# A buffer of its own for the early store, and one plan for both groups, in a top-2 dispatch kernel

## The chip, the cores and the metric

The kernel runs on one core of a Trainium2 chip. The metric is the time of one execution on the device in microseconds (us). Its data lie in the chip's main memory (DRAM); the core computes on its on-chip memory of 128 partitions. VectorE (DVE in the profile) does the element-wise arithmetic, ScalarE (ACT) the sigmoid. Transfers are issued by SyncE (SP) and ScalarE and carried by 16 DMA engines, which all of them share.

## The reference

There are 16 x 1024 = 16384 tokens, each with 512 values in `x` and 8 router logits, all 32-bit floats, and k is 2. Per token the two largest logits are taken, their softmax weights are normalised to sum to one, and the token's row is written out twice, once with each weight, the second largest first:

```python
    logits_max = np.max(router_logits, axis=-1, keepdims=True)
    probs = np.exp(router_logits - logits_max)
    probs = probs / np.sum(probs, axis=-1, keepdims=True)
    topk_indices = np.argsort(probs, axis=-1)[..., -k:]
    topk_probs = np.take_along_axis(probs, topk_indices, axis=-1)
    topk_probs = topk_probs / np.sum(topk_probs, axis=-1, keepdims=True)
    x_expanded = x[:, :, np.newaxis, :].repeat(k, axis=2)
    return (x_expanded * topk_probs[..., np.newaxis]).astype(np.float32)
```

So 33.6 MB of `x` and 0.5 MB of logits come in and 67.1 MB go out; the experts' indices are not returned. With two weights that sum to one, they are the sigmoids of plus and minus the difference of the two largest logits.

## The kernel before

**Tiling.** Each of the 128 partitions takes 128 tokens ("rows" from here on), in two groups of 65 and 63 rows (`GROUPS`, L49). A row of `x` is 2 KB per partition, a row of output 4 KB. The buffer `xs` (L95) holds one group of `x`, 65 rows; the buffer `osp` (L96) holds 16 rows of output (L = 16, h = 8). `logits` (L94) and the small tiles of the tournament in `top2_weights` have buffers of their own.

**Loads.** SyncE issues a group's loads in the pieces that `LOADS` gives (L112): 2, 4, 2, 8, 17 and 32 rows in the first group, 16, 16 and 31 in the second. After the first 6 rows it issues two loads of logits for both groups (L116, L117), and there the program puts the tournament: VectorE finds the largest and second largest of 8 logits by halving (L27 to L37), subtracts them (L40), and ScalarE makes the two weights (L42, L43).

**Multiplications and stores.** For each block of the plan VectorE multiplies `n` rows by their two weights into the block's output place (L128), and a DMA stores it (L136). In the first group the blocks are rows 0 to 1 and 2 to 15 in `osp`, 16 to 31 in `xs`, 32 to 39 and 40 to 47 in the halves of `osp`, then 48 to 56 and 57 to 64 in `xs` (`LAST`, L54). In the second: 0 to 15 in `osp`, 16 to 31 in `xs`, 32 to 39 and 40 to 47 in `osp`, 48 to 62 in `xs`. The block of two rows is stored from ScalarE's queue, "the early store", all others from SyncE's.

**Output written over the input.** A block that is "over" (L98 to L104) puts its output into `xs` itself, in the place of rows that have been used: n rows of output take the room of 2n rows of input. With `a = 2 * r - G` the place of rows 48 to 56 of group 0 is `xs[31:49]`, that of rows 57 to 64 is `xs[49:65]`; the second block (rows 16 to 31) is given G = 32, so it lies in `xs[0:32]`.

**Order.** There is no loop of fixed depth and no planner's due time: every engine and every queue takes its work in the order of the program, and a framework puts a wait wherever a region is read before it is written, written before it was read, or reused before its store has landed. A wait of SyncE holds up all transfers that are programmed behind it, and the second group's loads stand behind the first group's stores.

Of the kernel before, what the change touches and what calls it, by code (L numbers as in the profile page):

```python
# [1 line left out]

# [4 lines left out]

F32 = mybir.dt.float32
ALU = mybir.AluOpType
ACTF = mybir.ActivationFunctionType  # L10
P = 128


def top2_weights(nc, pool, logits, M, E, tag=""):

    hi, lo, n = None, None, E  # L20
    while n > 1:
        n //= 2
        if hi is None:
            a, b = logits[:, :, 0:n], logits[:, :, n : 2 * n]
            nhi = pool.tile([P, M, n], F32, tag=f"hi{n}{tag}")
            nlo = b
            nc.vector.tensor_tensor(nhi, a, b, op=ALU.max)  # L27
            nc.vector.tensor_tensor(nlo, a, b, op=ALU.min)  # L28
        else:
            a, b = hi[:, :, 0:n], hi[:, :, n : 2 * n]  # L30
            nhi = pool.tile([P, M, n], F32, tag=f"hi{n}{tag}")
            nlo = pool.tile([P, M, n], F32, tag=f"lo{n}{tag}")
            tmp = pool.tile([P, M, n], F32, tag=f"tmp{n}{tag}")
            nc.vector.tensor_tensor(tmp, lo[:, :, 0:n], lo[:, :, n : 2 * n], op=ALU.max)  # L34
            nc.vector.tensor_tensor(nlo, a, b, op=ALU.min)  # L35
            nc.vector.tensor_tensor(nlo, nlo, tmp, op=ALU.max)  # L36
            nc.vector.tensor_tensor(nhi, a, b, op=ALU.max)  # L37
        hi, lo = nhi, nlo
    dlt = pool.tile([P, M], F32, tag=f"dlt{tag}")
    nc.vector.tensor_tensor(dlt, hi[:, :, 0], lo[:, :, 0], op=ALU.subtract)  # L40
    WA = pool.tile([P, M, 2], F32, tag=f"WA{tag}")
    nc.scalar.activation(WA[:, :, 0], dlt, ACTF.Sigmoid, scale=-1.0)  # L42
    nc.scalar.activation(WA[:, :, 1], dlt, ACTF.Sigmoid, scale=1.0)  # L43
    return WA

GROUPS = [65, 63]  # L49

LOADS = [[2, 4, 2, 8, 17, 32], [16, 16, 31]]


LAST = [[(48, 9), (57, 8)], [(48, 15)]]  # L54


@with_exitstack
def kernel(
    ctx: ExitStack,
    tc: tile.TileContext,  # L60
    x: bass.AP,
    router_logits: bass.AP,
    k: bass.AP,
    out: bass.AP,
):
    nc = tc.nc
    B, S, D = x.shape
    E = router_logits.shape[-1]
    N = B * S
    assert int(k) == 2 and E == 8 and N == P * sum(GROUPS)  # L70
    M = N // P

    L = 16
    x_v, o_v, rl_v = [], [], []
    t0 = 0
    for n in GROUPS:
        t1 = t0 + P * n
        x_v.append(
            x.rearrange("b s d -> (b s) d")[t0:t1].rearrange("(p m) d -> p m d", p=P)
        )  # L80
        o_v.append(
            out.rearrange("b s k d -> (b s) k d")[t0:t1].rearrange(
                "(p m) k d -> p m k d", p=P
            )
        )
        rl_v.append(
            router_logits.rearrange("b s e -> (b s) e")[t0:t1].rearrange(
                "(p m) e -> p m e", p=P
            )
        )  # L90
        t0 = t1

    wpool = ctx.enter_context(tc.tile_pool(name="wpool", bufs=1))
    logits = wpool.tile([P, M, E], F32)  # L94
    xs = wpool.tile([P, max(GROUPS), D], F32)  # L95
    osp = wpool.tile([P, L, 2, D], F32)  # L96

    def over(r, n, G):  # L98

        a = 2 * r - G
        return xs[:, a : a + 2 * n, :].rearrange("p (r k) d -> p r k d", k=2)  # L104

    h = L // 2
    e = 2
    m0 = 0
    for g, G in enumerate(GROUPS):
        r = 0  # L110
        for n in LOADS[g]:
            nc.sync.dma_start(xs[:, r : r + n, :], x_v[g][:, r : r + n, :])  # L112
            r += n
            if g == 0 and r == 6:

                nc.sync.dma_start(logits[:, :G], rl_v[0])  # L116
                nc.sync.dma_start(logits[:, G:], rl_v[1])  # L117
                WA = top2_weights(nc, wpool, logits, M, E)
        assert r == G
        begin = [(0, e, osp[:, :e]), (e, L - e, osp[:, e:])] if g == 0 else [(0, L, osp)]  # L120
        plan = begin + [
            (L, L, over(L, L, 2 * L)),
            (2 * L, h, osp[:, :h]),
            (2 * L + h, h, osp[:, h:]),
        ]
        plan += [(r, n, over(r, n, G)) for r, n in LAST[g]]
        for r, n, og in plan:
            nc.vector.tensor_tensor(  # L128
                og,
                xs[:, r : r + n, :].unsqueeze(2).to_broadcast([P, n, 2, D]),  # L130
                WA[:, m0 + r : m0 + r + n, :].unsqueeze(3).to_broadcast([P, n, 2, D]),
                op=ALU.mult,
            )

            queue = nc.scalar if n == e else nc.sync
            queue.dma_start(o_v[g][:, r : r + n], og)  # L136
        m0 += G


# [1 line left out]
_INS = ['x', 'router_logits', 'k']  # L141
_OUTS = [((16, 1024, 2, 512), 'float32')]

_NUMBERS = {'k': 2}


# [26 lines left out]
```

## Time and profile before

| | |
|---|---|
| Three timed runs | 240.04, 240.05, 240.24 us; median 240.05 us |
| Profiled execution: its own time, as the page gives it (span) | 238.5 us |
| Median less this span (what lies around it) | 1.55 us |
| VectorE busy | 142.0 us, 60%, 23 instructions |
| of these, the multiplications (L128) | 69.1 us into `osp`, 69.1 us into `xs` |
| DMA packets | 3312, 101.19 MB, mean 424 GB/s over the span |
| Waits of VectorE for loads of `x` / for stores from `osp` / from `xs` | 31.2 / 30.1 / 2.0 us |

The page gives the span of the profiled execution, from its first instruction to its last, and no other time of that execution; the timed runs are other executions of the same kernel. The page cuts the span into 40 slices and gives for each the busy share of each engine in tenths, the mean busy share of the 16 DMA engines and what they moved. Transfers are listed by their queue: q1 holds those that SyncE issues, q10 the one that ScalarE issues. "To landing" is the time from the issue to the moment at which the last of a transfer's packets has arrived and its semaphore is set. A queue like SPq in the timeline shows the issuing instruction, not the movement of the data.

### The profile page before, as it was taken

The page shows a single profiled execution, that of the slowest core. Times are in us where ns is not written, and L with a number is a line of the kernel's source. Part 1 is how long each engine was busy: PE and PEld are TensorE (multiplying, and loading weights), DVE is VectorE, ACT ScalarE, POOL GpSimd, SP SyncE. Part 2 cuts the span into 40 slices and gives each one's busy share as a digit, 9 for nine tenths or more (in the row PEclk, how much of TensorE's full clock was granted, in tenths as well). Part 3 has the DMA queues.
Part 4 walks back from the last instruction along what each step waited for, and adds up shares of the span by engine and source line. Part 5 has one row for each costly group of instructions (what it writes and reads, how often), then busy time and mean ns, then how long its engine had stood idle before and what let it go on. Part 6 is the DMA issues. An engine that isn't in the chain of part 4 may idle for free.

```text
span 238.5 us, 116 instructions
## 1 busy us (share of the span) xinstructions
DVE 142.0 (60%) x23; ACT 1.8 (1%) x3; POOL 0.2 (0%) x4
## 2 busy tenths in 40 slices
DVE  0599999900299699900000699999006999990000
ACT  2000000000000000000000000000000000000000
POOL 0000000000000000000000000000000000000000
DMA  7999989899898999999999999998999989999994
GB/s 261 434 470 411 459 383 528 330 462 462 352 506 352 440 440 440 440 414 465 440 429 434 412 478 458 394 495 374 462 418 429 451 363 429 440 440 429 495 453 206
DMA packets 3312, 101.19 MB, mean 424 GB/s; under 512 B 368, under 2 KB 496, under 8 KB 880
## 3 DMA queue, kind: packets, MB, share of 16 engines
q1 hardware_dynamic: 3168, 100.14, 97.8%
q10 hardware_dynamic: 144, 1.05, 1.0%
HBM read 34.08 MB, written 67.11 MB: 424 GB/s over the span
## 4 chain that ended last, share of the span: by engine, by line
DMA 43%; DVE 41%; issue 4%; SPq 1%; ACT 0%; DVEq 0%
DVE xs L128 22%; DVE osp L128 18%; DMA out_dram<-xs 15%; DMA xs<-in_x_dram 13%; DMA out_dram<-osp 13%; DMA logits<-in_router_logits_dram 3%; SPq L112 0%; DVE nhi L27 0%; DVE logits L28 0%; DVE nlo L36 0%; DVE nhi L37 0%; DVE tmp L34 0%; DVE nlo L35 0%; SPq L116 0%; SPq L136 0%
## 5 line engine op out<-in xcount | busy, mean ns | idle before, releaser
L128 DVE TENSOR_TENSOR osp<-xs,WA 128x8192 f32<-128x8192 f32 (+3 forms) x7 | 69.1, 9908 | 61.9 <-DMA xs<-in_x_dram 31.2
L128 DVE TENSOR_TENSOR xs<-xs,WA 128x16384 f32<-128x16384 f32 (+3 forms) x5 | 69.1, 13812 | 2.2 <-DMA out_dram<-xs 2.0
L27 DVE TENSOR_TENSOR nhi<-logits 128x512 f32<-128x512 f32 x1 | 0.7, 691 | 8.3 <-DMA logits<-in_router_logits_dram 8.3
L42 ACT ACT_TABLE_LOAD x1 | 1.3, 1283 | 0.7 <-PEq L154 0.7
L28 DVE TENSOR_TENSOR logits<-logits 128x512 f32<-128x512 f32 x1 | 0.7, 692 | 0.0
L37 DVE TENSOR_TENSOR nhi<-nhi 128x256 f32<-128x256 f32 (+1 forms) x2 | 0.7, 351 | 0.0
L35 DVE TENSOR_TENSOR nlo<-nhi 128x256 f32<-128x256 f32 (+1 forms) x2 | 0.7, 350 | 0.0
L36 DVE TENSOR_TENSOR nlo<-nlo,tmp 128x256 f32<-128x256 f32 (+1 forms) x2 | 0.7, 350 | 0.0
L34 DVE TENSOR_TENSOR tmp<-logits 128x256 f32<-128x256 f32 x1 | 0.4, 418 | 0.0
L42 ACT ACTIVATE WA<-dlt 128x128 f32<-128x128 f32 x1 | 0.3, 315 | 10.2 <-DVE dlt L40 10.2
L40 DVE TENSOR_TENSOR dlt<-nhi,nlo 128x128 f32<-128x128 f32 x1 | 0.3, 291 | 0.0
L43 ACT ACTIVATE WA<-dlt 128x128 f32<-128x128 f32 x1 | 0.3, 297 | 0.0
L34 DVE TENSOR_TENSOR tmp<-nlo 128x128 f32<-128x128 f32 x1 | 0.3, 283 | 0.0
L154 POOL MEMSET const-bfloat16-1.0<- 128x1 bf16 x1 | 0.1, 101 | 0.0
L154 POOL MEMSET const-uint8-127<- 128x1 uint8 x1 | 0.1, 101 | 0.0
L154 POOL MEMSET const-float32-0.0<- 128x1 f32 x1 | 0.1, 98 | 0.2 <-issue 0.2
L154 POOL MEMSET const-float32-1.0<- 128x1 f32 x1 | 0.1, 98 | 0.0
## 6 DMA issues: line engine op xcount, KB each, us to landing
out_dram<-osp SPq DMA_DIRECT2D x4, 4096.0 KB, 20.7
xs<-in_x_dram SPq DMA_DIRECT2D x2, 4096.0 KB, 29.9
xs<-in_x_dram SPq DMA_DIRECT2D x1, 7936.0 KB, 38.0
out_dram<-xs SPq DMA_DIRECT2D x1, 7680.0 KB, 23.2
out_dram<-osp SPq DMA_DIRECT2D x1, 7168.0 KB, 33.9
out_dram<-xs SPq DMA_DIRECT2D x1, 4608.0 KB, 20.4
xs<-in_x_dram SPq DMA_DIRECT2D x1, 4352.0 KB, 22.4
out_dram<-xs SPq DMA_DIRECT2D x1, 4096.0 KB, 21.5
```

What stands on the lines that cost most here:

```text
L27: nc.vector.tensor_tensor(nhi, a, b, op=ALU.max)
L28: nc.vector.tensor_tensor(nlo, a, b, op=ALU.min)
L34: nc.vector.tensor_tensor(tmp, lo[:, :, 0:n], lo[:, :, n : 2 * n], op=ALU.max)
L35: nc.vector.tensor_tensor(nlo, a, b, op=ALU.min)
L36: nc.vector.tensor_tensor(nlo, nlo, tmp, op=ALU.max)
L37: nc.vector.tensor_tensor(nhi, a, b, op=ALU.max)
L40: nc.vector.tensor_tensor(dlt, hi[:, :, 0], lo[:, :, 0], op=ALU.subtract)
L42: nc.scalar.activation(WA[:, :, 0], dlt, ACTF.Sigmoid, scale=-1.0)
L43: nc.scalar.activation(WA[:, :, 1], dlt, ACTF.Sigmoid, scale=1.0)
L128: nc.vector.tensor_tensor(og, xs[:, r : r + n, :].unsqueeze(2).to_broadcast([P, n, 2, D]), WA[:, m0 + r : m0 + r + n, :].unsqueeze(3).to_b ...
L154: nc = _bacc.Bacc("TRN2", target_bir_lowering=False, num_devices=1)
```

## The change

It touches buffers, the cut of the first group's loads, and the plan of the first group's blocks.

- The early store's two rows are written to a new buffer `oe` of two rows. `EARLY = [2, 0]` says how many such rows a group has; `LAST` is gone.
- The other 63 rows of the first group have the blocks of the second group, moved by two: rows 2 to 17 in all 16 rows of `osp`, 18 to 33 in `xs`, 34 to 41 and 42 to 49 in the halves of `osp`, 50 to 64 in `xs`, which makes six stores instead of seven.
- `over` gives its block the place `xs[r - n : r + n]`: `xs[2:34]` for rows 18 to 33, `xs[35:65]` for rows 50 to 64. In the second group the places are those of before.
- The first group's loads are 2, 4, 2, 10, 15 and 32 rows instead of 2, 4, 2, 8, 17 and 32.
- `logits` and the tournament's small tiles are cut out of the front of `osp` by `room`; `dlt` and `WA` have buffers of their own. The tournament's instructions are the same.

```diff
-LOADS = [[2, 4, 2, 8, 17, 32], [16, 16, 31]]
+LOADS = [[2, 4, 2, 10, 15, 32], [16, 16, 31]]
-LAST = [[(48, 9), (57, 8)], [(48, 15)]]
+EARLY = [2, 0]
...
-    logits = wpool.tile([P, M, E], F32)
     xs = wpool.tile([P, max(GROUPS), D], F32)
     osp = wpool.tile([P, L, 2, D], F32)
-    def over(r, n, G):
-        a = 2 * r - G
-        return xs[:, a : a + 2 * n, :].rearrange("p (r k) d -> p r k d", k=2)
+    oe = wpool.tile([P, max(EARLY), 2, D], F32)
+    WA = wpool.tile([P, M, 2], F32)
+    dlt = wpool.tile([P, M], F32)
+    flat = osp.rearrange("p l k d -> p (l k d)")
+    taken = [0]
+    def room(n):
+        o = taken[0]
+        taken[0] += M * n
+        return flat[:, o : o + M * n].rearrange("p (m n) -> p m n", n=n)
+    logits = room(E)
+    def over(r, n):
+        return xs[:, r - n : r + n, :].rearrange("p (r k) d -> p r k d", k=2)
...
-                WA = top2_weights(nc, wpool, logits, M, E)
+                top2_weights(nc, WA, dlt, room, logits, E)
...
-        begin = [(0, e, osp[:, :e]), (e, L - e, osp[:, e:])] if g == 0 else [(0, L, osp)]
-        plan = begin + [
-            (L, L, over(L, L, 2 * L)),
-            (2 * L, h, osp[:, :h]),
-            (2 * L + h, h, osp[:, h:]),
+        e = EARLY[g]
+        plan = [(0, e, oe, nc.scalar)] if e else []
+        plan += [
+            (e, L, osp, nc.sync),
+            (e + L, L, over(e + L, L), nc.sync),
+            (e + 2 * L, h, osp[:, :h], nc.sync),
+            (e + 2 * L + h, h, osp[:, h:], nc.sync),
+            (e + 3 * L, G - e - 3 * L, over(e + 3 * L, G - e - 3 * L), nc.sync),
         ]
-        plan += [(r, n, over(r, n, G)) for r, n in LAST[g]]
-        for r, n, og in plan:
+        for r, n, og, queue in plan:
...
-            queue = nc.scalar if n == e else nc.sync
             queue.dma_start(o_v[g][:, r : r + n], og)
```

More of the change, by code (lines that the diff above doesn't have):

```diff
@@ L11, with top2_weights @@
 P = 128
-def top2_weights(nc, pool, logits, M, E, tag=""):
+def top2_weights(nc, WA, dlt, room, logits, E):
+    tt = nc.vector.tensor_tensor
     hi, lo, n = None, None, E
@@ L24, in top2_weights @@
             a, b = logits[:, :, 0:n], logits[:, :, n : 2 * n]
[L25 to L28, printed above, removed]
+            nhi, nlo = room(n), b
+            tt(nhi, a, b, op=ALU.max)
+            tt(nlo, a, b, op=ALU.min)
         else:
             a, b = hi[:, :, 0:n], hi[:, :, n : 2 * n]
[L31 to L37, printed above, removed]
+            nhi, nlo, tmp = room(n), room(n), room(n)
+            tt(tmp, lo[:, :, 0:n], lo[:, :, n : 2 * n], op=ALU.max)
+            tt(nlo, a, b, op=ALU.min)
+            tt(nlo, nlo, tmp, op=ALU.max)
+            tt(nhi, a, b, op=ALU.max)
         hi, lo = nhi, nlo
-    dlt = pool.tile([P, M], F32, tag=f"dlt{tag}")
-    nc.vector.tensor_tensor(dlt, hi[:, :, 0], lo[:, :, 0], op=ALU.subtract)
-    WA = pool.tile([P, M, 2], F32, tag=f"WA{tag}")
+    tt(dlt, hi[:, :, 0], lo[:, :, 0], op=ALU.subtract)
     nc.scalar.activation(WA[:, :, 0], dlt, ACTF.Sigmoid, scale=-1.0)
     nc.scalar.activation(WA[:, :, 1], dlt, ACTF.Sigmoid, scale=1.0)
-    return WA
 GROUPS = [65, 63]
-LOADS = [[2, 4, 2, 8, 17, 32], [16, 16, 31]]
-LAST = [[(48, 9), (57, 8)], [(48, 15)]]
+LOADS = [[2, 4, 2, 10, 15, 32], [16, 16, 31]]
+EARLY = [2, 0]
 @with_exitstack
@@ L93 @@
     wpool = ctx.enter_context(tc.tile_pool(name="wpool", bufs=1))
-    logits = wpool.tile([P, M, E], F32)
     xs = wpool.tile([P, max(GROUPS), D], F32)
     osp = wpool.tile([P, L, 2, D], F32)
-    def over(r, n, G):
-        a = 2 * r - G
-        return xs[:, a : a + 2 * n, :].rearrange("p (r k) d -> p r k d", k=2)
+    oe = wpool.tile([P, max(EARLY), 2, D], F32)
[10 more added lines that the diff above has]
+        return xs[:, r - n : r + n, :].rearrange("p (r k) d -> p r k d", k=2)
     h = L // 2
-    e = 2
     m0 = 0
```

## The prediction

> **What bounds the kernel now.** I first read the page's slices and queues, to see which resource has no holes.
>
> ```profile
> DMA  7999989899898999999999999998999989999994
> GB/s 261 434 470 411 459 383 528 330 462 462 352 506 352 440 440 440 440 414 465 440 429 434 412 478 458 394 495 374 462 418 429 451 363 429 440 440 429 495 453 206
> q1 hardware_dynamic: 3168, 100.14, 97.8%
> q10 hardware_dynamic: 144, 1.05, 1.0%
> ```
>
> The reader is to see that the 16 DMA engines are full in every slice but the first and the last: the packets of q1 (SyncE's queue) and q10 (ScalarE's) fill 98.8% of the span. VectorE is busy for only 60%. All 101.19 MB go through those engines whatever the order, so the end moves only if an engine runs dry, or if the packets get slower. The chain of waits, with its 41% DVE, misleads here: it names who released whom, not what was scarce.
>
> Next the waits of VectorE, to know its slack.
>
> ```profile
> DVE osp L128 <- DMA xs<-in_x_dram: 31.2, 1, 31.2
> DVE osp L128 <- DMA out_dram<-osp: 30.1, 2, 16.7
> DVE xs L128 <- DMA out_dram<-xs: 2.0, 1, 2.0
> ```
>
> These 63.3 us are VectorE waiting for a transfer while the queue is full, so removing one is worth nothing by itself. The question is how late VectorE may hand over each store before the queue drains; that I read from the timeline.
>
> ```profile
> 0.73 0.86 SPq L112 DMA_DIRECT2D xs<-in_x_dram  x2
> 2.58 2.22 SPq L112 DMA_DIRECT2D xs<-in_x_dram  x4
> 12.75 17.29 DVE L128 TENSOR_TENSOR osp<-xs,WA 128x2048 f32<-128x2048 f32 x2 [0.58 <-ACT WA L43]
> 15.08 0.37 ACTq L136 DMA_DIRECT2D out_dram<-osp  x1
> 30.07 0.35 SPq L136 DMA_DIRECT2D out_dram<-osp  x1
> 30.08 17.23 DVE L128 TENSOR_TENSOR xs<-xs,WA 128x16384 f32<-128x16384 f32 x1
> 47.33 0.34 SPq L136 DMA_DIRECT2D out_dram<-xs  x1
> 64.02 17.29 DVE L128 TENSOR_TENSOR osp<-xs,WA 128x8192 f32<-128x8192 f32 x2 [16.71 <-DMA out_dram<-osp]
> ```
>
> The store of rows 2 to 15 is issued at 30.07 and the next at 47.33. Last come the issues by size, and stretches of 0.1 us (start and end, length, busy times, clock, DMA share, GB/s), in which a packet counts whole where it starts.
>
> ```profile
> xs<-in_x_dram SPq DMA_DIRECT2D x1, 42.6
> ```
>
> ```profile
> 1.70:1.80 0.10, 0.00 (x0) 0.10 (x1) 0.00 (x0) 1.00 1.47 205
> 43.20:43.30 0.10, 0.10 (x1) 0.00 (x0) 0.00 (x0) 1.00 13.30 4588
> 43.30:43.40 0.10, 0.10 (x1) 0.00 (x0) 0.00 (x0) 1.00 5.86 1966
> 43.40:43.50 0.10, 0.10 (x1) 0.00 (x0) 0.00 (x0) 1.00 7.81 2621
> 43.50:43.60 0.10, 0.10 (x1) 0.00 (x0) 0.00 (x0) 1.00 3.77 1311
> ...
> 46.10:46.20 0.10, 0.10 (x1) 0.00 (x0) 0.00 (x0) 1.00 1.33 573
> ...
> 46.60:46.70 0.10, 0.10 (x1) 0.00 (x0) 0.00 (x0) 1.00 2.66 1147
> ```
>
> Each transfer is 128 packets, 8 for each engine, so the engines move in waves of 16. The last wave of the 32-row load starts between 43.2 and 43.6; its shares add up to 30.74 tenths of a us, 3.07 us for each packet. The first wave of the store behind it starts between 46.1 and 46.7. The queue is thus served in order, without a gap. The load was the last of the four issues that end at 4.80 (2.58 + 2.22), so it was issued near 4.37 and landed near 46.97, 0.3 us after its last packet.
>
> **The change part by part.** The sums are made on the profiled execution, with its span of 238.5 us. The three timed runs have a median of 240.05 us, 1.55 us more, which lies around the span; I add the difference in span to the median.
>
> *Scratch and logits in the buffer osp.* The same 11 VectorE instructions on the same shapes (0.28 to 0.69 us each, 8.28 to 12.17): no cost. Were the shared buffer to bring waits between them, at worst an instruction's length each, about 4.5 us, the chain would end near 17; that delays the first big store from about 32.9 to 37.4, and the load keeps the queue full until 46. Nothing either way.
>
> *Two rows to a buffer of their own.* The 2.29 us instruction and the ScalarE store at 15.08 stay. Nobody waits for this store any more; before, the instruction at 64.02 did, beside the later store that ended its wait. Nothing.
>
> *Loads of 10 and 15 rows for 8 and 17.* As many DMAs. The 8-row load landed near 14.3 (11.0 us after an issue near 3.4); two rows more, 0.52 MB at 434 GB/s, put the 10-row load at 15.5. The next multiplication starts 0.5 us later than 15.04. It now has 16 rows (17.23 us by the 128x16384 row) instead of 14 (15.09), so its store is issued at 32.8 and not at 30.07. The cover is again the load, to 46.1. Nothing.
>
> *One store fewer.* Seven stores of group 0 become six: 9 and 8 rows turn into one of 15, 14 into 16, 8 + 8 stay. The bytes are equal. What goes is 8 packets and a semaphore packet on every engine. From the waves in the trace (64 KB packets 2.416 us, those of an 8-row store at 83.6 to 84.2 1.214) a packet costs 2 x 1.214 - 2.416 = 0.012 us beyond its bytes: 8 x 0.012, about 0.1 us gained. SyncE issues one 0.33 us DMA less, off the path.
>
> *The 2.0 us wait at 83.3 goes.* The last block, xs[35:65], no longer overlaps the earlier in-place block, xs[2:34]. The queue was full there, so nothing; group 1's first loads are issued near 100 and no longer at 102.30 and near 113, behind a queue that is full to 122. Nothing.
>
> *A new wait.* This is the one that matters. The second 16-row block was rows 16 to 31 and is now rows 18 to 33. The loads end at rows 2, 6, 8, 18, 33, 65: row 33 comes with the 32-row load, where before row 31 came with the 17-row one. The 17.23 us instruction that started at 30.08 now waits until 46.97. Behind it on VectorE are all other multiplications of the group, behind its store on SyncE all other stores. It starts 0.09 us after the landing (as 83.27 to 83.36 in the chain), ends at 64.29, and SyncE issues at 64.30 instead of 47.33.
>
> What is in the queue until then: the 16-row store, issued at 32.8, starts at 46.1 to 46.7 and has 8 waves. A wave of 64 KB packets costs 2.41 us (those of the present 16-row store start at 63.1, 65.5 and 67.9), 19.3 in all, so the engines run dry between 65.4 and 66.0. When does the new store's data start? The lower bound is the first load on this same SyncE queue: issued at 0.73, first packets at 1.70, 0.97 us, and 14 packets within 0.35 us. The upper bound is ScalarE's store, issued at 15.08, whose first packet shows at 18.6, 3.5 us; but there the engines were busy with packets of 1.26 us, of which one or two lay ahead. I take 0.97, since the queue and the idle engine match. Data starts from 65.27 on the first engine to 65.62 on the last. The engine that drains first idles up to 0.2 us, the one that drains last, which sets the end, has 0.4 to 0.7 us to spare. Cost 0 to 0.2 us at 0.97; at 3.5 us data starts at 67.8, and the slowest engine loses 1.8 us.
>
> The Trainium skill's page "DMA: Bandwidth & Descriptors", section "Anatomy of one DMA", speaks against this hand-over: it gives a DMA a fixed cost of about 2.0 us, mostly at its completion. The trace has 0.3 + 0.97 = 1.3 us for landing and start here, 0.7 less. By the page an estimate puts the data near 66.0 and the cost at 0.3 us; by the row it is 0.1.
>
> Afterwards the queue has cover again: the next 8-row block waits for the first big store (66.4), is issued at 75.1, and the store begun at 65.6 lasts to 85. The last 15-row store goes out at 99.9 with 8-row stores queued to 104.8. Group 1 has the same plan, and its first load, queued behind the same bytes, lands as before. Sum: +0.2 - 0.1 = +0.1 us; predicted 240.2 us.
>
> **The rivals.**
>
> *The queue runs dry (slower).* Place: 65.4 to 67.8. It decides once a store needs more than about 1.7 us from issue to data (0.97 plus the slowest engine's spare 0.7); each us beyond that is a us at the end, as no later stretch is idle enough to win it back. ScalarE's 3.5 us speak for it, the first load's 0.97 against. At 3.5 us the end moves by 1.8 (less 0.1): 241.8; midway, at 2.5 us, 0.8 less 0.1: 240.8.
>
> *The stretched wave disappears (faster).* The last wave of the 32-row load took 3.07 us, its predecessor (40.8) 2.42, and the last one of group 1's load (158.0) about 2.4. If the 0.65 us comes from the sizes queued around it, the new load sizes and the 16-row store may lose it: 239.4. Against it: this load and the store's kind stay.
>
> *The change does less than it says.* If the wait for row 33 were not there, nothing would be left but the 0.1 us: 240.0. The overlap of one row is real in the data, so I give it little.
>
> *VectorE becomes the bound.* Its group-0 work would end at 99.9 instead of 101.86, with 63 us of waits still in the kernel: no change, 240.2.
>
> **How the numbers follow.** About 0.2%, 0.48 us, is what a measurement of this kernel can tell from no change. The cover holds or nearly so, with the two no-change rivals: 0.51, at 240.2, its own range 239.8 to 240.5. The queue runs dry by more than 0.5 us: 0.36, from 240.6 to 241.8. The stretched wave goes: 0.13, 239.4. The range 239.4 to 241.6 leaves out the top of the second case and what I have not thought of.
>
> **What would show it.** Right: VectorE waits about 14 us for an x load before 47, SyncE's second big store is issued near 64.3, the 2.0 us wait is gone, the DMA engines stay full from 64 to 68, and the end is within 0.3 us of the old. Wrong: a hole of half a us or more in the DMA stretches between 65 and 68, or waves there longer than 2.42 us; or the wave at 43 back at 2.42 with an earlier end.

## The result, and the profile after

The changed kernel takes 243.25 us (median of four runs, 242.49 to 243.43), the kernel before beside it 240.15 us (240.04 to 240.34). The ratio is 1.0114, with a 95% interval from 1.0098 to 1.013: slower by 1.1%, about 3 us. Predicted were 240.2 us, with a range up to 241.6. The profiled execution of the changed kernel took 243.43 us, 241.6 of them its span, against a span of 238.5 before.

The page's slices and queues, as they were read of the kernel before:

```profile
DMA  7999999898989899999969999999999998999974
GB/s 257 445 420 437 453 472 423 347 521 347 521 347 521 347 434 434 434 412 488 488 271 429 434 465 462 483 341 391 477 391 477 401 466 374 429 434 479 478 336 183
q1 hardware_dynamic: 3024, 100.14, 97.2%
q10 hardware_dynamic: 144, 1.05, 1.0%
```

The same 101.19 MB in a longer span. No slice around 65 us, which the prediction watched, shows a hole. The 21st slice (120.8 to 126.9 us) has only 6 tenths and 271 GB/s, but that is no hole either: the page counts a packet whole where it starts, and the long packets that start at 120.2 to 120.6 us count in the slice before. Taken by the time in which packets run, the engines are 99% busy in it. The queues' shares tell more: 98.2% of 241.6 us is 237.3 us of packets for each engine, where 98.8% of 238.5 us was 235.6 us. So the packets got 1.6 us longer, and the engines stand idle 1.5 us more; in the slices' true busy time this idling lies in the last one (0.49 busy, before 0.73).

The waits of VectorE and the timeline up to the second group's loads:

```profile
DVE osp L129 <- DMA xs<-in_x_dram: 35.5, 2, 34.8
DVE osp L129 <- DMA out_dram<-osp: 16.9, 2, 14.8
DVE xs L129 <- DMA xs<-in_x_dram: 14.2, 1, 14.2
```

```profile
32.96 0.35 SPq L135 DMA_DIRECT2D out_dram<-osp  x1
47.13 17.23 DVE L129 TENSOR_TENSOR xs<-xs,WA 128x16384 f32<-128x16384 f32 x1 [14.20 <-DMA xs<-in_x_dram]
64.39 0.34 SPq L135 DMA_DIRECT2D out_dram<-xs  x1
66.42 17.29 DVE L129 TENSOR_TENSOR osp<-xs,WA 128x8192 f32<-128x8192 f32 x2 [2.06 <-DMA out_dram<-osp]
75.14 8.93 SPq L135 DMA_DIRECT2D out_dram<-osp  x2
83.75 16.16 DVE L129 TENSOR_TENSOR xs<-xs,WA 128x15360 f32<-128x15360 f32 x1
99.93 0.33 SPq L135 DMA_DIRECT2D out_dram<-xs  x1
```

The 14.2 us wait for row 33 is there, and the 2.0 us wait of before is gone. The late store is issued at 64.39. Up to 100 us every time of this list that the prediction named is within 0.2 us of it.

Then stretches of the trace (start and end, length, busy times of the engines, clock, DMA share, GB/s), each cut so that it holds the starts of one wave of 16 packets, one for each engine. A packet counts whole where it starts, so share times length is the mean time of a packet, and GB/s times length the bytes of the wave. First the kernel before, then the changed one:

```profile
121.00:121.80 0.80, 0.00 (x0) 0.00 (x0) 0.00 (x0) 1.00 1.52 655
158.00:158.80 0.80, 0.80 (x1) 0.00 (x0) 0.00 (x0) 1.00 3.03 1270
234.20:235.00 0.80, 0.00 (x0) 0.00 (x0) 0.00 (x0) 1.00 2.83 1229
```

```profile
63.00:63.80 0.80, 0.80 (x1) 0.00 (x0) 0.00 (x0) 1.00 3.02 1311
65.40:66.20 0.80, 0.00 (x0) 0.00 (x0) 0.00 (x0) 1.00 3.04 1311
120.00:120.80 0.80, 0.00 (x0) 0.00 (x0) 0.00 (x0) 1.00 3.67 1229
158.70:160.40 1.70, 1.70 (x1) 0.00 (x0) 0.00 (x0) 1.00 1.90 598
235.70:236.50 0.80, 0.00 (x0) 0.00 (x0) 0.00 (x0) 1.00 2.48 1075
236.50:238.00 1.50, 0.00 (x0) 0.00 (x0) 0.00 (x0) 1.00 0.00 0
238.00:238.20 0.20, 0.00 (x0) 0.00 (x0) 0.00 (x0) 1.00 1.43 614
```

At the hand-over there is no hole: the last wave of the first big store starts from 63.0 on with packets of 2.42 us (3.02 x 0.80), and the late store's first wave follows at 65.4 with 2.43 us. The time is lost at the two *turns*, the places where the queue goes over from stores to loads and from loads to stores. The last wave ahead of the second group's loads takes 2.94 us a packet (3.67 x 0.80), where the same 60 KB take 2.26 at the end of the kernel before (2.83 x 0.80); before the change the last wave at this place took its regular 1.22. The last wave of the second group's loads takes 3.23 us (1.90 x 1.70) against 2.42 (3.03 x 0.80) before. Behind the first turn the engines are also no longer in step: in the very last wave 14 packets start from 235.7 to 236.5 and two only after 238.0 (614 GB/s x 0.2 us is two packets of 60 KB), where before all 16 start within 0.8 us, from 234.2 on. These two set the end, and the other engines idle beside them.

The chain of waits says the same in its way. Before, then after:

```profile
102.30 30.61 DMA xs<-in_x_dram
```

```profile
100.31 34.30 DMA xs<-in_x_dram
```

The second group's first load is issued 2.0 us earlier and lands 1.7 us later (134.61 against 132.91).

### The profile page after: what moved, and what is told of

Same layout as the page of the kernel before. It is cut to its first block, busy times and chain, and to the rows that moved or that the text cites. A ratio compares the mean times of both kernels' runs of the same rounds, so it can differ in the third digit from the quotient of the medians.

```text
span 241.6 us, 111 instructions
## 1 busy us (share of the span) xinstructions
DVE 141.9 (59%) x22; ACT 1.8 (1%) x3; POOL 0.2 (0%) x4
## 2 busy tenths in 40 slices
DMA packets 3168, 101.19 MB, mean 419 GB/s; under 512 B 352, under 2 KB 480, under 8 KB 864
## 4 chain that ended last, share of the span: by engine, by line
DMA 46%; DVE 38%; issue 4%; SPq 1%; DVEq 0%
DMA out_dram<-osp 27%; DVE osp L129 25%; DMA xs<-in_x_dram 19%; DVE xs L129 13%; SPq L112 1%; SPq L116 0%; SPq L115 0%; SPq L135 0%; DVEq L129 0%
## 5 line engine op out<-in xcount | busy, mean ns | idle before, releaser
L129 DVE TENSOR_TENSOR osp<-xs,WA 128x8192 f32<-128x8192 f32 (+1 forms) x6 | 69.0, 11533 | 52.3 <-DMA xs<-in_x_dram 35.5
L129 DVE TENSOR_TENSOR xs<-xs,WA 128x16384 f32<-128x16384 f32 (+1 forms) x4 | 66.8, 16692 | 14.3 <-DMA xs<-in_x_dram 14.2
L26 DVE TENSOR_TENSOR osp<-osp 128x512 f32<-128x512 f32 x1 | 0.7, 693 | 8.3 <-DMA osp<-in_router_logits_dram 8.3
L129 DVE TENSOR_TENSOR oe<-xs,WA 128x2048 f32<-128x2048 f32 x1 | 2.3, 2293 | 0.6 <-ACT WA L38 0.6
L27 DVE TENSOR_TENSOR osp<-osp 128x512 f32<-128x512 f32 x1 | 0.7, 692 | 0.0
L32 DVE TENSOR_TENSOR osp<-osp 128x256 f32<-128x256 f32 (+1 forms) x2 | 0.7, 350 | 0.0
L31 DVE TENSOR_TENSOR osp<-osp 128x256 f32<-128x256 f32 (+1 forms) x2 | 0.7, 350 | 0.0
L34 DVE TENSOR_TENSOR osp<-osp 128x256 f32<-128x256 f32 (+1 forms) x2 | 0.7, 350 | 0.0
L33 DVE TENSOR_TENSOR osp<-osp 128x256 f32<-128x256 f32 (+1 forms) x2 | 0.7, 350 | 0.0
```

Source lines behind the costliest of these rows:

```text
L26: tt(nhi, a, b, op=ALU.max)
L27: tt(nlo, a, b, op=ALU.min)
L31: tt(tmp, lo[:, :, 0:n], lo[:, :, n : 2 * n], op=ALU.max)
L32: tt(nlo, a, b, op=ALU.min)
L33: tt(nlo, nlo, tmp, op=ALU.max)
L34: tt(nhi, a, b, op=ALU.max)
```

## The experiments

In every series the kernel before was run beside the others; its medians were 240.15 to 240.32 us. Single runs of it came near 242 too: of the 98 beside the experiments nine lie above 241.5 us (241.75 to 242.23), five of them among the 27 of one series. So a median and the list of runs say more here than one run. "Lead" below is the time from the issue of the late store to the moment at which the first engine has nothing left ahead of it, read from the one profiled execution of each kernel.

### What is to blame: the last store's size, or the late hand-over?

The first theory after the result was the size of packets at the turns (A), the second the late hand-over (B). Four kernels tell them apart.

Split the last store of the changed kernel, multiplication untouched:

```diff
-            queue.dma_start(o_v[g][:, r : r + n], og)
+            if g == 0 and n == 15:
+                queue.dma_start(o_v[g][:, r : r + 7], og[:, :7])
+                queue.dma_start(o_v[g][:, r + 7 : r + n], og[:, 7:])
+            else:
+                queue.dma_start(o_v[g][:, r : r + n], og)
```

> The changed kernel, but the 15-row block that ends the first group is stored as two DMAs of 7 and 8 rows instead of one of 15; the multiplication stays whole. Theory A (the size of the last packets before the queue turns from stores to loads: 60 KB packets stretch from 2.27 to 2.93 us at 120.3 in the changed kernel, the 32 KB packets of before don't): the stretched wave goes, no engine falls behind there, and the time comes to 240.2 to 241.0 us. Theory B (the late hand-over, the wait for row 33, costs it all): nothing changes, 243.2 us.

Measured: 243.1 us (242.81 to 243.74), ratio 1.0125 (1.0103 to 1.0148). Nothing is gained with 32 KB packets at the turn; their last wave ahead of the loads stretches as well, to 1.92 us where 1.21 is regular.

Give the kernel before the 15-row store:

```diff
-LAST = [[(48, 9), (57, 8)], [(48, 15)]]
+LAST = [[(48, 2), (50, 15)], [(48, 15)]]
...
-            queue = nc.scalar if n == e else nc.sync
+            queue = nc.scalar if r == 0 and n == e else nc.sync
```

> The kernel before, but its last two blocks of the first group, 9 and 8 rows, are cut into 2 and 15 rows, so that the last store ahead of the second group's loads has 60 KB packets as in the changed kernel; everything else, the wait-free row 33 among it, stays. Theory A: the wave ahead of the loads stretches by about 0.65 us, engines fall behind, and the time comes to 241 to 243.4 us. Theory B: 240.1 us as before.

Measured: 240.15 us, ratio 0.9998 (0.9989 to 1.0007). Its last wave ahead of the loads:

```profile
120.00:120.80 0.80, 0.00 (x0) 0.00 (x0) 0.00 (x0) 1.00 2.83 1229
```

2.26 us (2.83 x 0.80) for 60 KB: no stretch. Theory A falls with these two runs.

Take only the wait for row 33 out of the changed kernel:

```diff
-LOADS = [[2, 4, 2, 10, 15, 32], [16, 16, 31]]
+LOADS = [[2, 4, 2, 10, 16, 31], [16, 16, 31]]
```

> The changed kernel, but the fifth and sixth load have 16 and 31 rows instead of 15 and 32, so that row 33 comes with the fifth and the second 16-row block need not wait until 47. Theory A: the wait was covered by the queue; 243.2 us as changed. Theory B: the loss goes, 240.1 us.

Measured: 240.66 us, ratio 1.0027 (1.0004 to 1.0049), with single runs of 241.83 and 242.75. The late store is now issued at 49.98. From 66.42 to 100.31 VectorE and SyncE do the same things within 0.02 us as in the changed kernel, and the two turns look like this:

```profile
119.90:120.70 0.80, 0.00 (x0) 0.00 (x0) 0.00 (x0) 1.00 2.83 1229
157.80:158.60 0.80, 0.80 (x1) 0.00 (x0) 0.00 (x0) 1.00 2.78 1190
```

2.26 us for 60 KB, and for 62 KB 2.37 (2.78 x 0.80 over the 15 of 16 packets that start in this stretch): regular, or nearly so. So the wait is what costs nearly all of the 3 us, though it leaves no hole where it occurs; the median stays 0.45 us above the kernel before.

Smaller last loads in the kernel before, against the 3.07 us wave at 43 us:

```diff
-LOADS = [[2, 4, 2, 8, 17, 32], [16, 16, 31]]
+LOADS = [[2, 4, 2, 8, 17, 16, 16], [16, 16, 15, 16]]
```

> The kernel before, but the last load of each group is cut in two: 16 + 16 rows for 32, 15 + 16 rows for 31, so that the last packets ahead of the stores are 32 KB. Theory A: the wave that took 3.07 us ahead of the first stores loses its 0.65 us of stretch, 239.5 us. Theory B, and every theory in which the stretch belongs to the turn of direction whatever the packet: 240.1 us, or 0.1 to 0.2 more for two DMAs more.

Measured: 240.28 us, ratio 1.0002 (0.9993 to 1.0012). The last 32 KB wave ahead of the stores takes 1.41 us where 1.21 is regular, so the stretch at that turn shrinks from 0.65 to 0.2 us, and the end gains nothing.

### The same hand-over in the kernel before, and how late is late

Make the second 16-row block of the kernel before wait as late as in the changed one:

```diff
-LOADS = [[2, 4, 2, 8, 17, 32], [16, 16, 31]]
+LOADS = [[2, 4, 2, 8, 15, 30, 4], [16, 16, 31]]
```

> The kernel before, with the first group's loads cut as 2, 4, 2, 8, 15, 30 and 4 rows. Row 31 then comes with the 30-row load near 44.6, so the second 16-row block ends near 61.9 and its store is issued about 1.1 us before the 14-row store ahead of it drains at 63.1: the same just-in-time hand-over as in the changed kernel, nothing else of the change. Theory C (a store handed over while only the packet in progress is left ahead of it costs nothing there, but makes the later turns between stores and loads slow): 242.3 to 243.5 us, with the stretched waves near 122 and 160. Theory D (the loss belongs to other parts of the changed plan, or to chance at the turns): 240.1 to 240.4 us.

Measured: 242.71 us (six runs, 242.34 to 243.06), ratio 1.0093 (1.0064 to 1.0122). Hand-over and turns:

```profile
60.70:61.50 0.80, 0.72 (x1) 0.00 (x0) 0.00 (x0) 1.00 2.65 1147
62.80:63.60 0.80, 0.00 (x0) 0.00 (x0) 0.00 (x0) 1.00 3.05 1311
120.90:121.80 0.90, 0.00 (x0) 0.00 (x0) 0.00 (x0) 1.00 1.93 583
158.70:160.70 2.00, 2.00 (x1) 0.00 (x0) 0.00 (x0) 1.00 1.37 508
```

The store is issued at 61.45, its first wave follows the last of the store ahead of it without a hole (62.8; 60.7 plus 2.12), and 58 us later the 32 KB wave at the first turn takes 1.74 us instead of 1.22, the one at the second 2.74 instead of 2.42. Nothing else of the change is in this kernel.

Then the changed kernel with its 32-row load cut, so that row 33 comes earlier by steps:

```diff
-LOADS = [[2, 4, 2, 10, 15, 32], [16, 16, 31]]
+LOADS = [[2, 4, 2, 10, 15, 28, 4], [16, 16, 31]]
```

> The changed kernel with its 32-row load cut into 28 and 4 rows: row 33 lands near 44.7, the store is issued near 62.0, 3.5 us ahead of the drain at 65.5, with one whole packet for each engine still waiting ahead of it. Theory C with a sharp edge at the last packet: 240.2 to 240.9 us. A loss that grows with the lateness of the store: 242.2 to 242.8 us, four fifths of the changed kernel's. Theory D: 243.2 us.

Measured: 240.15 us, ratio 0.9991 (0.9966 to 1.0017); the store went out at 61.30. One run of the ten took 241.83 us.

With 20 and 12 rows:

> The changed kernel with its 32-row load cut into 20 and 12 rows: row 33 lands near 39.8, the store is issued near 57.1, 8.3 us ahead of the drain. Theory C: 240.2 to 240.9 us. A loss that grows with the lateness: 241.5 to 241.9 us. Theory D: 243.2 us.

Measured: 240.26 us, ratio 0.9986 (0.9959 to 1.0013); the store went out at 56.56.

With 31 rows and 1:

> The changed kernel with its 32-row load cut into 31 and 1 rows, so that row 33 lands somewhat over a us earlier and the store is issued near 63.0, about 2.4 us ahead of the drain at 65.5, when most engines are just beginning the last packet ahead of it. Theory C with an edge at the last packet: between the two levels, or runs at both, 240.2 to 243.2 us. A loss proportional to the missing time: 242.9 us.

Measured: four runs from 240.26 to 240.64, six from 242.34 to 243.14, and nothing between (ratio of all 1.0054, 1.0021 to 1.0087); the store went out at 63.55. In the profiled execution, one of the lower four, the first engine drained at 65.57. Put in order of lead, with the share of runs above 241.5 us:

| kernel | store issued | first engine drained | lead | above 241.5 us |
|---|---|---|---|---|
| changed | 64.39 | 65.5 | 1.1 us | 4 of 4 |
| changed, last store split | 64.27 | 65.4 | 1.2 us | 4 of 4 |
| before, late hand-over | 61.45 | 62.9 | 1.5 us | 6 of 6 |
| changed, 31 and 1 | 63.55 | 65.6 | 2.0 us | 6 of 10 |
| changed, 28 and 4 | 61.30 | 65.4 | 4.1 us | 1 of 10 |
| changed, 20 and 12 | 56.56 | 65.4 | 8.8 us | 0 of 10 |
| changed, row 33 in the fifth load | 49.98 | 65.5 | 15.5 us | 2 of 10 |
| before | 47.33 | 63.1 | 15.8 us | 9 of 98 |

The loss does not grow with lateness. There are two levels some 2 us apart. At a lead of 1.5 us or less every run is on the upper one, at 2.0 us six of ten, and from 4.1 us on no more than in the kernel before, as far as ten runs of each can tell. Where between 2.0 and 4.1 us the edge lies was not measured.

### Where it is paid

A late hand-over behind the last turn, in the kernel before:

```diff
-LAST = [[(48, 9), (57, 8)], [(48, 15)]]
+LAST = [[(48, 9), (57, 8)], [(47, 16)]]
...
-            (2 * L + h, h, osp[:, h:]),
+            (2 * L + h, h - g, osp[:, h : 2 * h - g]),
```

> The kernel before with its very last two blocks cut into 7 and 16 rows instead of 8 and 15. The last block lies in xs[31:63] then, waits for the store of xs[0:32] (landed near 199.5) and ends near 216.7, so the last store is issued 0.5 to 1.2 us before the queue ahead of it drains (near 217.2 to 217.9): a just-in-time hand-over like the changed kernel's, but with no turn between stores and loads behind it. Theory C, that such a hand-over is paid at the later turns: 240.1 to 240.8 us (the upper end is half a us of dry queue). If it were paid at the hand-over, or by every later packet: 242 us or more.

Measured: 240.85 us, ratio 1.0024 (1.0008 to 1.0039). The store was issued at 217.41, while the engines were ending their last packets (1.06 us each, begun from 216.1 to 216.7):

```profile
216.10:216.70 0.60, 0.60 (x1) 0.00 (x0) 0.00 (x0) 1.00 1.66 717
217.41:218.20 0.79, 0.00 (x0) 0.00 (x0) 0.00 (x0) 1.00 0.01 0
218.20:218.40 0.20, 0.00 (x0) 0.00 (x0) 0.00 (x0) 1.00 12.28 5243
```

No data packet starts from the issue to 218.20, 0.8 us later; then all 16 start within 0.2 us. The first of them had drained at 217.2 (216.1 plus 1.06), 0.2 us ahead of the issue, so this store came too late for a just-in-time hand-over: the queue ran dry. The engines stood still for 0.5 to 1.0 us and the kernel lost 0.6, with no second price behind it. A hand-over with 1 us of lead and no turn behind it was not run. That the 2.4 us of the late kernel before are paid at the turns is read from its waves: up to 100 us no packet behind the hand-over takes more than 0.05 us over its regular time.

A queue that runs dry in the changed kernel, by storing 14 of the 16 rows ahead of the late store and two behind it:

```diff
-            queue.dma_start(o_v[g][:, r : r + n], og)
+            if g == 0 and r == e:
+                queue.dma_start(o_v[g][:, r : r + 14], og[:, :14])
+            else:
+                queue.dma_start(o_v[g][:, r : r + n], og)
+            if g == 0 and r == e + L:
+                queue.dma_start(o_v[g][:, e + 14 : e + L], osp[:, 14:])
```

> The changed kernel, but of the first 16-row block in osp only 14 rows are stored at once; the other two rows are stored after the second 16-row block's store. The queue ahead of the late store (issued near 64.4, data near 65.3) then drains at 63.1 to 63.6, so the engines stand still for 1.7 to 2.2 us. If the slow turns follow from any store that is not well ahead of the drain: 240.1 + 1.9 + 2.6, about 244.6 us. If they follow only from a hand-over while the last packet is in progress, and engines that have stopped start clean: 241.9 to 242.4 us.

Measured: 244.89 us, ratio 1.0188 (1.0171 to 1.0205). It does not tell what it should: the store of two rows held back the next multiplication into `osp` (14.7 us of wait), and SyncE's order changed so that a load of the second group went out at 96.76, between two stores, which makes two more turns. What it shows cleanly is the hole: no packet starts from 63.6 to 65.2. And engines that have stopped don't start clean: the last wave ahead of the loads near 106 us takes 1.96 us and the last one ahead of the next store, near 117, 1.83, where 32 KB take 1.21; only the turn at 163 us is regular again (2.38 us).

### Is the first load's issue the link?

In the profiles of the changed kernel, of its split-store kernel and of the late kernel before, one more thing differs: the first transfer issued behind a deep queue near 100 us keeps SyncE for 1.24 to 1.26 us. In the profiled executions without the loss this takes 0.41 (15-row store in the kernel before) to 1.10 us (31 and 1, an execution of the lower level). Two kernels ask whether that is a cause. The late hand-over in the plan with the shortest issue (`LAST` of 2 and 15 rows with the loads 2, 4, 2, 8, 15, 30, 4):

> The kernel before with the late hand-over (loads 2, 4, 2, 8, 15, 30, 4) and with its last two blocks of the first group cut into 2 and 15 rows; with those blocks alone the issue of the second group's first load took 0.41 us, the shortest of all. If the late hand-over is enough by itself: 242.3 to 243.1 us, as with 9 and 8 rows. If the long issue of that load is the link and the two-row store shortens it: 240.1 to 240.6 us, with an issue below 1 us.

Measured: 242.59 us, ratio 1.0086 (1.0069 to 1.0104). The late store, and the issue of the load:

```profile
61.33 0.34 SPq L136 DMA_DIRECT2D out_dram<-xs  x1
102.17 1.24 SPq L112 DMA_DIRECT2D xs<-in_x_dram  x1
```

The issue that took 0.41 us without the late hand-over takes 1.24 with it. The hand-over leads to both, the long issue and the loss. In the kernel whose queue ran dry the first two turns are slow although no issue of SyncE near them takes more than 0.45 us, so the long issue isn't needed for slow turns.

The early hand-over with the split store (the first experiment's split with the loads 2, 4, 2, 10, 16, 31):

> The changed kernel with row 33 in the fifth load (16 and 31 rows), so that the hand-over is early, and with the store of the 15-row block split into 7 and 8 rows, as in the split kernel that ran in 243.1 us. If the late hand-over is needed for the loss: 240.2 to 240.9 us. If four or five transfers queued when the loads are issued are enough: 242.5 us or more.

Measured: 240.42 us, ratio 1.0008 (0.9995 to 1.0022). The same queue at 100 us without the late hand-over: no loss, but for one run of 241.52 us.

### What is left, and a repair

Row 33 early, and the last block as two blocks of 7 and 8 rows, each multiplied and stored by itself:

```diff
+        if g == 0:
+            plan += [(50, 7, over(50, 7 + 8)[:, :7], nc.sync), (57, 8, over(57, 8), nc.sync)]
+        else:
+            plan += [(48, 15, over(48, 15), nc.sync)]
```

> The changed kernel with row 33 in the fifth load (16 and 31 rows), and the 15-row block that ends the first group cut into two blocks of 7 and 8 rows, each multiplied and stored by itself. If what is left of the loss without the wait for row 33 (240.66 us, up to 242.75) comes from the 15-row store behind a short queue: 240.2 us, and no run over 240.6. If it comes from elsewhere: 240.6 us.

Measured: 240.49 us, ratio 1.0008 (0.9978 to 1.0038), with runs of 241.43 and 242.37. Whether the occasional runs above 241 are rarer than with one block can't be said from ten runs.

One early row instead of two, which moves the second 16-row block to rows 17 to 32 and so out of the 32-row load:

```diff
-EARLY = [2, 0]
+EARLY = [1, 0]
```

> The changed kernel with one early row instead of two. The blocks are rows 1 to 16, 17 to 32, 33 to 40, 41 to 48 and 49 to 64, so that the second 16-row block ends at row 32, the last row of the fifth load, and does not wait for the 32-row load; loads are as in the changed kernel. Theory C: the loss is gone with the plan otherwise unchanged, 240.0 to 240.7 us. Theory D: 243.2 us.

Measured: 240.36 us, all ten runs from 240.30 to 240.85, ratio 0.9999 (0.9983 to 1.0014). The second block starts at once and its store is issued at 50.02:

```profile
32.77 17.23 DVE L129 TENSOR_TENSOR xs<-xs,WA 128x16384 f32<-128x16384 f32 x1
50.02 0.34 SPq L135 DMA_DIRECT2D out_dram<-xs  x1
```

Its lead is 14.6 us (the first engine drains at 64.6). With this one figure the new plan equals the kernel before. No kernel of the study was measurably faster than it.

## Why the prediction was wrong

**Right.** The DMA engines are what is scarce, and VectorE's waits alone cost nothing. Scratch in `osp`, the buffer of the early store, the cut of the loads and the store fewer cost nothing that could be measured: with the wait removed by one early row, all of them together run at the time of before. The new wait for row 33 was named as the one part that matters, with its times (landing 46.97, issue 64.30, next block at 66.4, issues at 75.1 and 99.9; the trace has 64.39, 66.42, 75.14 and 99.93).

**Right, at its place.** "Data starts from 65.27 on the first engine to 65.62 on the last ... Cost 0 to 0.2 us": the trace shows no hole at 65. The start of 0.97 us, taken from the first load, was if anything too long: the store at the kernel's end shows 0.8 us. That the 3.5 us of ScalarE's store were mostly packets lying ahead fits this, but was not tested. The Trainium skill's page "DMA: Bandwidth & Descriptors", section "Anatomy of one DMA — SWDGE (gpsimd) path", gives its fixed cost of about 2.0 us for transfers that GpSimd issues, which the prediction did not say; this store is SyncE's. The estimate worked out from it (data near 66.0) came out too late by half a us: the late store's first packets start at 65.5.

**Wrong.** The step that failed is the sentence behind it: "Afterwards the queue has cover again ... Group 1 has the same plan, and its first load, queued behind the same bytes, lands as before." It landed 1.7 us later, and the end came 3.1 us later. The sum put the later turns at nothing: it took it as given that packets are served at one rate as long as the queue holds something, though the prediction itself had named slower packets as a way to move the end. In the kernel before that is so but for the turn at 43 us; with a store handed over 1.1 us ahead of the drain it is no longer so at the two later turns, where the packets lost 0.7 and 0.8 us in the mean. That is half of the 3.1 us. The other half is a way that the prediction did not list: some engines fell 1.5 us behind the others, and the last of them set the end.

The rival "the queue runs dry" was on the right side and named the right store, but its price was wrong in kind: it put the price at 65 to 68 us and the edge at the point where an engine has nothing to do. The edge lies earlier, and the price is paid 55 and 95 us later. The rival "the stretched wave disappears" had a stretched wave at a turn before it, at 43 us, in the kernel before; I priced only its going away, and did not ask why another turn could not get one.

**Open.** What the engines carry from the hand-over to the turns is not shown. That they carry something is, and from the hand-over on, in the lengths of the packets. Of the packets that start from 66.5 to 100 us, in the middle of the stores, each takes exactly 2.418 us (64 KB) or 1.213 us (32 KB) in all eleven profiled executions below 241.5 us, 3598 packets, the lower-level one of 31 and 1 among them. In the changed kernel 29 of 320 take 3 to 30 ns more, in its split-store kernel 77 of 320, in the two late kernels before 72 and 66 of 336, in the one that ran dry 195 of 288. These nanoseconds are not the loss, but they mark it from 68 to 73 us on, ahead of the long issue near 100 us and of the first turn. Why single runs of kernels with an early hand-over reach the upper level too is open as well; none of them was profiled.

## What to carry to other kernels

Where the DMA queue is the bound, look at how far ahead of the drain each transfer is issued, and keep that lead at several us (4.1 us and more had at most two runs in ten above 241.5 us here, the kernel before nine in 98); "not yet dry" is not enough. After moving a block by a row or two, check which load its *last* row comes with: one row of 34 in the next load cost 14 us of wait, and one early row less took it away. And compare turns between loads and stores wave by wave, since a loss can lie far behind its cause.

## What the runs showed of the hardware

- In the profiled executions below 241.5 us an engine's store packets are regular to the ns from 66.5 to 100 us (64 KB in 2.418 us, 32 KB in 1.213), but the last wave ahead of a turn can stretch: by 0.65 us at 43 us in the kernel before, by 1.1 us there in the kernel with one early row (3.53 us against 2.42), and by 0.36 us at 158 us in the lower-level execution of 31 and 1, none of which has the loss, and by 0.7 to 0.9 us over the regular time at both later turns in the changed one.
- A store issued to idle engines has its first packets 0.8 us after the start of the issue (217.41 to 218.2 us at the kernel's end, 64.37 to 65.2 in the one that ran dry).
- A store handed over 1.1 to 1.7 us ahead of the drain put the kernel on the upper level in 14 of 14 runs of three kernels (the changed one 4, the late kernel before 6, the late one with 2 and 15 rows 4) and in all four of the split store; in the profiled execution of each, the turns 55 to 95 us later are slow. At 2.0 us it was 6 of 10, with two clear levels.
- The same late hand-over lengthens an issue on SyncE 40 us later from 0.41 to 1.24 us, with the same transfers in the queue; in the eleven profiled executions below 241.5 us the first issue of this kind takes 0.41 to 1.10 us.
